# Three products of a swapped projection added in one place, as 256-column matmuls

## The chip, the cores and the metric

The kernel runs on 1 core of one Trainium2 chip. The metric is the device time of one execution in microseconds (us). Before the change it is 2711.26 us, the median of 3 runs (2711.25 to 2711.56).

## The reference, cut to what matters

Two transformer blocks over 256 tokens of width 2048 in float32, one after the other, with a norm between them:

```
x = x + gla(rmsnorm(x)) ; x = x + (relu(rmsnorm(x) @ w_up)**2) @ w_down      # block 1, hidden width 8192
x = rmsnorm(x)
proj = rmsnorm(x) @ w_in_2          # q k v | xr gr | sc_b sc_c sc_x | three gates of 2048
x = x + (g_a*attention + g_b*lru + g_c*shortconv) @ w_out
x = x + (relu(rmsnorm(x) @ w_up_2)**2) @ w_down_2 ; x = rmsnorm(x)
```

Nearly all arithmetic is in the projections, matrix products with weights that are read once from HBM, 499.5 MB in all.

## The kernel before, in words

**Products.** TensorE multiplies in float32r. A float32 operand is split into hi, its rounding to float32r, and lo, what is left; a product is x_hi w_hi + x_hi w_lo + x_lo w_hi. An activation tile holds for each 128-feature group the hi of 256 tokens and then the lo of 256 tokens, side by side and transposed.

**Jobs.** A job is one block of 512 output columns. Its weights stream in chunks of 512 features by 512 columns (1 MB, issued on SP's queue at L181); each chunk is two halves of 256 features. For each half ACT writes hi (`wh`, L204) and DVE lo (`wl`, L205), up to three halves ahead of TensorE. `run()` walks over all halves of all jobs in program order and calls `products()` for each.

**Plain and swapped jobs.** A plain job holds the activations stationary and streams 512 weight columns: for each feature group and each 128 tokens three matmuls of 512 columns, two of them in a row with the same stationary tile. A swapped job holds the weights stationary and streams the activations, so that its output comes out with its 512 columns on the partitions, in four blocks of 128. For each block and each feature group it issues two matmuls: `wh` against hi and lo together (512 columns: x_hi w_hi in the left half of a bank, x_lo w_hi in the right), and `wl` against hi alone (256 columns, added to the left half). A job has four blocks and 16 feature groups, so 64 such pairs. There are 50 swapped jobs: 4 in block 1's mixer (q and k), 16 in each MLP's first projection, 14 in block 2 (short convolution 6, recurrence 4, attention q and k 4). That makes 3200 pairs.

**PSUM.** Accumulators (`acc`) are whole banks, six in rotation: a swapped job takes four, a plain one two. Two more banks serve side work.

**Side work.** Norms, gates, scans and attention are generators that advance one step after each half. A swapped job's generator begins with `g_sum` (L301): for each block ACT copies the right half of the bank to SBUF (L304) and DVE adds it to the left half (L305). What follows depends on the job; in the MLP it is relu and square in one DVE instruction (L608), then the split into hi and lo (L612, L616).

Every engine works through its own queue in program order; all matmuls of the projections have one line (L212).

Of the kernel before, what the change touches and what calls it, by code (L numbers as in the profile page):

```python
# [8 lines left out]
F32 = mybir.dt.float32  # L9
F32R = mybir.dt.float32r  # L10
AF = mybir.ActivationFunctionType
ALU = mybir.AluOpType
# [4 lines left out]
KB = 512  # L17
# [5 lines left out]
NSLOT = 26  # L23


# Every projection runs as a stream of weight tiles through TensorE in float32r.  A float32 operand is
# split exactly into hi = round(w) and lo = round(w - hi); a product is x_hi w_hi + x_hi w_lo + x_lo w_hi.
# An activation tile holds, for two 128-feature groups, [hi of 256 tokens | lo of 256 tokens], transposed.
# A plain job multiplies with the activations stationary and returns [token, 512 columns] in two banks; a
# swapped job holds the weights stationary and returns its columns on partitions, [column, (hi sum | lo sum)].  # L30
# Side work (norms, gates, scans, attention) is written as generators that advance between weight tiles.
class Job:
    def __init__(self, w, kts, act, ev, key, need=None, pre=None, swap=False):
        self.w, self.kts, self.act, self.ev, self.key, self.swap = w, kts, act, ev, key, swap
# [4 lines left out]
def two_blocks(tc, A, out):  # L39
    nc = tc.nc  # L40
    es = ExitStack()
    with es:
# [27 lines left out]
        def flat(ap):  # L70
            return ap.rearrange("p a b -> p (a b)")

        # side work -------------------------------------------------------
        active, gens = [], {}

        def start(key, gen):
# [35 lines left out]
                    drain(rec[1])  # L112
                advance(rec)

        # constants -------------------------------------------------------
        xres = cp.tile([128, 2, D], F32, name="xres")
        cst = cp.tile([128, 128], F32, name="cst")
        ident = cst
# [29 lines left out]
            o = offB[n] + kt  # L148
            return colB[:, o:o + 1]

        # weight stream ---------------------------------------------------
        jobs = []
        chunks, halves = [], []
        st = {"dma": 0, "split": 0}
# [53 lines left out]
                if st["dma"] - ci <= RAW:  # L208
                    dma_chunk()

        def mm(o, l, r, a, b):
            PE.matmul(o, l, r, start=a, stop=b)  # L212

        def products(j, acc, x, wh, wl, first, last, toks=(0, 1)):
            if j.swap:
                for n in range(4):
                    c = slice(n * 128, (n + 1) * 128)
                    for i in range(2):
                        mm(acc[n], wh[:, i, c], flat(x[i]), first and i == 0, False)
                        mm(acc[n][:, 0:256], wl[:, i, c], x[i][:, 0, :], False, last and i == 1)  # L220
            else:
                for i in range(2):
                    a, b = first and i == 0, last and i == 1
                    for t in toks:
                        xh = x[i][:, 0, t * 128:(t + 1) * 128]
                        xl = x[i][:, 1, t * 128:(t + 1) * 128]
                        mm(acc[t], xh, wh[:, i], a, False)
                        mm(acc[t], xh, wl[:, i], False, False)
                        mm(acc[t], xl, wh[:, i], False, b)

        def run():
            acc = None
            for s in range(len(halves)):
                j, ci, h, ks, is_first, is_last = halves[s]
                for k in ks:
                    for key in j.need(k):
                        drain(key)
                if is_first:
                    if j.pre:
                        j.pre()  # L240
                    acc = [ps.tile([128, KB], F32, name="acc", tag="acc", bufs=6) for _ in range(4 if j.swap else 2)]
                look = min(LOOK, 1 + s // 3)
                while st["split"] <= min(s + look, len(halves) - 1):
                    split_half()
                if s == len(halves) - 4:
                    for t in range(2):
                        for q in range(s, s + 4):
                            products(j, acc, [j.act(k) for k in halves[q][3]], *whs[q], False, halves[q][5], (t,))
                        j.ev(acc, t)
                    break  # L250
                wh, wl = whs.pop(s)
                products(j, acc, [j.act(k) for k in ks], wh, wl, is_first, is_last)
                if is_last:
                    start(j.key, j.ev(acc))
                tick()
            while active:
                tick()

        # helpers ---------------------------------------------------------
        def pair_transpose(src, pr, name="tp"):  # L260
            tp = tpt([128, 2, 256], name)
            for i in range(2):
# [35 lines left out]
                if pr == 0:  # L298
                    yield 0

        def g_sum(acc, dst):  # L301
            for n in range(4):
                r = t1("right")
                ACT.activation(r, acc[n][:, 256:512], AF.Copy)  # L304
                V.tensor_tensor(dst[:, n, :], acc[n][:, 0:256], r, op=ALU.add)  # L305

        def over4(ap):
            return ap[:, None, :].to_broadcast([128, 4, 256])
# [48 lines left out]
            T[name] = cp.tile([128, 2, 4], F32, name=name)  # L357
            return T[name]

        # ================= block 1 =======================================  # L360
        w_in = A["gla_w_in"][0]
        xd = A["x"][0].rearrange("(t p) d -> p t d", p=128)

# [31 lines left out]
        def ev_q(hf):  # L395
            def f(acc):
                q = T["qT", hf] = slot([128, 4, 256], F32, "qT")
                g_sum(acc, q)
                yield ("rs1",)
                V.tensor_tensor(q, q, over4(R1q), op=ALU.mult)  # L400
            return f
# [77 lines left out]
        def ev_k(hf):  # L479
            def f(acc):  # L480
                k = T["kT", hf] = slot([128, 4, 256], F32, "kT")
                g_sum(acc, k)
                yield ("glow",)
                V.tensor_tensor(k, k, T["E"][hf], op=ALU.mult)
            return f
# [109 lines left out]
            job(A["gla_w_out"][0], n * KB, 16, acts("o1"), ev_out1(n), ("out1", n), lambda k: (("r", k // 4),))  # L595
        stats("ss2"), keep("rs2", 2), keep("rs2q", 2)

        # ================= mlp ===========================================
        def mlp(tag, w_up, w_down, xname, xkeys, rskey, rsq, ev_last):
            for hf in range(2):  # L600
                for jn in range(8):
                    def ev(acc, hf=hf, jn=jn):
                        y = slot([128, 4, 256], F32, "up")
                        g_sum(acc, y)
                        yield 0
                        for p in range(2):
                            v = flat(y[:, 2 * p:2 * p + 2, :])
                            V.scalar_tensor_tensor(v, v, 0.0, v, op0=ALU.max, op1=ALU.mult)  # L608
                        yield 0
                        for p in range(2):  # L610
                            d = T[tag, hf, 2 * jn + p] = act_tile("h")
                            ACT.activation(d[:, :, 0, :], y[:, 2 * p:2 * p + 2, :], AF.Copy)  # L612
                        yield 0
                        for p in range(2):
                            d = T[tag, hf, 2 * jn + p]
                            V.tensor_tensor(d[:, :, 1, :], y[:, 2 * p:2 * p + 2, :], d[:, :, 0, :].bitcast(F32), op=ALU.subtract)  # L616
                    job(w_up, hf * 4096 + jn * KB, 16, acts(xname), ev, (tag + "up", hf, jn),
                        (lambda k: ((xkeys, k // 4),)) if hf == 0 and jn == 0 else None, swap=True)
                for n in range(4):
                    def lhs(k, hf=hf):  # L620
                        return T[tag, hf, k // 2][:, k % 2]
                    if hf == 0:
                        def ev(acc, n=n):
                            drain(rskey)
                            for t in range(2):
                                V.scalar_tensor_tensor(xblk(t, n), acc[t], rsq[:, t:t + 1], xblk(t, n), op0=ALU.mult, op1=ALU.add)
                            yield 0
                    else:
                        ev = ev_last(n)
                    job(w_down[hf * 4096:(hf + 1) * 4096, :], n * KB, 32, lhs, ev, (tag + "dn", hf, n),  # L630
                        (lambda k, hf=hf: ((tag + "up", hf, k // 4),)) if n == 0 else None,
                        pre=pre_dn.get((tag, hf, n)))
# [42 lines left out]

        mlp("m1", A["mlp_w_up"][0], A["mlp_w_down"][0], "x2", "out1", "rs2", T["rs2q"], ev_last1)

        # ================= block 2 =======================================
        w2 = A["w_in_2"][0]
        X3 = acts("x3")  # L680
        r12 = T["r12"]
# [12 lines left out]
        def ev_cols(name, scale):  # L694
            def f(acc):
                d = slot([128, 4, 256], F32, "col")
                T[name] = d
                g_sum(acc, d)
                yield ("r12",)
                if scale:  # L700
                    V.tensor_tensor(d, d, over4(T[scale]), op=ALU.mult)
            return f

        def ev_sx(b):
            def f(acc):
                bs, cx = T["sb", b], T["sc", b]
                xs = slot([128, 4, 256], F32, "xs")
                g_sum(acc, xs)
                yield ("sc", b)
                yield ("sb", b)  # L710
                V.tensor_tensor(flat(cx), flat(cx), flat(xs), op=ALU.mult)
# [48 lines left out]
        def ev_xr(b):  # L760
            def f(acc):
                xs = slot([128, 4, 256], F32, "xs")
                g_sum(acc, xs)
                yield ("r12",)
                V.tensor_tensor(xs, xs, over4(T["R12"]), op=ALU.mult)
                xc = T["xc", b] = slot([128, 4, 256], F32, "xc")
# [37 lines left out]
        def ev_gr(b):  # L804
            def f(acc):
                gs = slot([128, 4, 256], F32, "gs")
                g_sum(acc, gs)
                yield ("r12",)
                V.tensor_tensor(gs, gs, over4(T["R12"]), op=ALU.mult)
                yield 0  # L810
# [220 lines left out]

        mlp("m2", A["w_mlp_up_2"][0], A["w_mlp_down_2"][0], "x5", "out2", "rs5", T["rs5q"], ev_last2)

        # ================= go ============================================
        plan()
        V.memset(ones, 1.0)
        make_identity(nc, ident)
# [76 lines left out]
```

## Time and profile before

| | |
|---|---|
| median of 3 runs | 2711.26 us |
| profiled execution, first to last instruction (span) | 2709.5 us |
| mean granted TensorE clock | 0.999 of full |
| TensorE matmul (PE) busy | 2696.5 us, 13389 matmuls |
| TensorE weight load (PEld) busy | 2264.6 us, 13389 loads |
| VectorE (DVE) busy | 1601.2 us |
| ScalarE (ACT) busy | 1256.7 us |
| DMA | 511.12 MB, 189 GB/s |

The page gives the profiled execution by its span; the 1.8 us up to the median are outside the first and last instruction. An engine's busy time is the union of its instructions' recorded intervals. Matmuls are pipelined, so a matmul's recorded duration overlaps the next one's: what a matmul costs in a stream is the distance from its start to the next start. A group's row has the line, engine, operation, output<-inputs, shape and count, then busy time, mean duration of one, and the idle time of the engine before it.

### The profile page before, as it was taken

What the parts mean: (1) busy time and instruction counts of PE and PEld (TensorE: products, weight loads), DVE (VectorE), ACT (ScalarE), POOL (GpSimd) and SP (SyncE); (2) the same over time, 40 slices, a digit from 0 to 9 for tenths busy, and PEclk for the clock granted to TensorE, in tenths of its full rate; (3) what the DMA queues carried; (4) which work ended last, traced back from release to release, by engine and by line L of the source; (5) the groups of instructions that cost most, each with busy time, mean ns of one, the idle gap of its engine ahead of it and who ended that gap; (6) DMA issues with size and microseconds to landing.
All of it is one profiled execution on the core that took longest, in us unless ns stands there. A gap on an engine that the chain in (4) does not pass through costs nothing.

```text
span 2709.5 us, 33062 instructions
## 1 busy us (share of the span) xinstructions
PE 2696.5 (100%) x13389; PEld 2264.6 (84%) x13389; DVE 1601.2 (59%) x1958; ACT 1256.7 (46%) x1581; POOL 20.0 (1%) x44
## 2 busy tenths in 40 slices
PE   9999999999999999999999999999999999999998
PEld 8877888888888888888888888888888888888887
DVE  6565655664456655667787556555556654466554
ACT  6444555443344444444555444444454443344443
POOL 0000000000000000000000000000000000000000
PEclk9999999999999999999999999999999999999999
DMA  7454555556565655665556555565555555556564
GB/s 238 156 174 152 175 186 185 186 187 200 188 188 186 201 194 187 201 214 185 185 193 219 187 182 182 193 196 187 186 187 186 187 188 200 187 187 202 188 200 140
DMA packets 256402, 511.12 MB, mean 189 GB/s; under 512 B 10524, under 2 KB 11208, under 8 KB 256120
## 3 DMA queue, kind: packets, MB, share of 16 engines
q1 hardware_dynamic: 253672, 499.50, 56.4%
q0 software_dynamic: 2576, 9.50, 1.1%
q8 instruction: 105, 1.72, 0.3%
q14 instruction: 49, 0.40, 0.0%
HBM read 506.86 MB, written 3.68 MB: 188 GB/s over the span
## 4 chain that ended last, share of the span: by engine, by line
PE 99%; DMA 1%; DVE 0%; issue 0%; ACT 0%; SPq 0%; DVEq 0%; ACTq 0%
PE acc L212 96%; PE tp L264 1%; DMA raw<-in_gla_w_in 0%; PE sc L212 0%; PE po L212 0%; PE gate L212 0%; PE as L212 0%; PE ao L212 0%; DMA xres<-in_x 0%; PE z L212 0%; PE tg L212 0%; PE pT L942 0%; DVE wl L205 0%; DVE oh L549 0%; ACT wh L204 0%
## 5 line engine op out<-in xcount | busy, mean ns | idle before, releaser
L205 DVE TENSOR_TENSOR wl<-raw,wh 128x1024 fp32r<-128x1024 f32 x942 | 1151.5, 1224 | 1019.6 <-ACT wh L204 1016.6
L204 ACT ACTIVATE wh<-raw 128x1024 fp32r<-128x1024 f32 x942 | 996.9, 1059 | 1260.3 <-PE acc L212 1208.9
L212 PE MATMUL acc<-a,wh 128*128 128x512 f32 x3200 | 1135.9, 400 | 0.2 <-DVE a L286 0.2
L212 PE MATMUL acc<-a,wl 128*128 128x256 f32 x3200 | 898.9, 281 | 0.3 <-DVE wl L205 0.3
L212 PEld LDWEIGHTS acc<-a,wh 128*128 128x128 f32 x3200 | 601.9, 188 | 150.7 <-ACT wh L204 0.7
L212 PE MATMUL acc<-wh,h 128*128 128x512 f32 x2048 | 632.9, 389 | 0.0
L212 PE MATMUL acc<-wh,a 128*128 128x512 f32 x1920 | 615.8, 395 | 0.0
L212 PEld LDWEIGHTS acc<-a,wl 128*128 128x128 f32 x3200 | 604.9, 189 | 1.0 <-DVE wl L205 0.6
L212 PEld LDWEIGHTS acc<-wh,h 128*128 128x128 f32 x2048 | 384.5, 188 | 79.8
L212 PEld LDWEIGHTS acc<-wh,a 128*128 128x128 f32 x1920 | 360.4, 188 | 80.0 <-issue 5.3
L212 PE MATMUL acc<-wl,h 128*128 128x512 f32 x1024 | 398.4, 389 | 0.0
L212 PE MATMUL acc<-wl,a 128*128 128x512 f32 x960 | 374.0, 390 | 0.0
L212 PEld LDWEIGHTS acc<-wl,h 128*128 128x128 f32 x1024 | 192.3, 188 | 39.6
L212 PEld LDWEIGHTS acc<-wl,a 128*128 128x128 f32 x960 | 180.4, 188 | 37.7 <-issue 1.9
L304 ACT ACTIVATE right<-acc 128x256 f32<-128x256 f32 x200 | 75.8, 379 | 43.1 <-PE acc L212 42.6
L285 ACT ACTIVATE a<-tp,colB 128x256 fp32r<-128x256 f32 x64 | 29.8, 466 | 43.9 <-DVE a L286 43.9
L305 DVE TENSOR_TENSOR up<-acc,right 128x256 f32<-128x256 f32 x128 | 48.1, 418 | 1.4
L608 DVE SCALAR_TENSOR_TENSOR up<-up 128x512 f32<-128x512 f32 x64 | 41.2, 684 | 0.0
L616 DVE TENSOR_TENSOR h<-up,h 128x512 fp32r<-128x512 f32 x64 | 41.1, 684 | 0.0
L286 DVE SCALAR_TENSOR_TENSOR a<-tp,colB,a 128x256 fp32r<-128x256 f32 x64 | 30.8, 481 | 17.4 <-ACT a L285 17.4
L212 PE MATMUL acc<-wh,yl 128*128 128x512 f32 x128 | 40.9, 393 | 0.0
L212 PE MATMUL acc<-wh,yc 128*128 128x512 f32 x128 | 40.7, 393 | 0.0
(253 smaller groups left out, 928.8 us busy)
## 6 DMA issues: line engine op xcount, KB each, us to landing
raw<-in_w_in SPq DMA_DIRECT2D x112, 1024.0 KB
raw<-in_mlp_w_up SPq DMA_DIRECT2D x64, 1024.0 KB
raw<-in_mlp_w_down SPq DMA_DIRECT2D x64, 1024.0 KB
raw<-in_w_mlp_up SPq DMA_DIRECT2D x64, 1024.0 KB
raw<-in_w_mlp_down SPq DMA_DIRECT2D x64, 1024.0 KB
raw<-in_gla_w_in SPq DMA_DIRECT2D x46, 1024.0 KB
raw<-in_gla_w_out SPq DMA_DIRECT2D x16, 1024.0 KB
raw<-in_w_out SPq DMA_DIRECT2D x16, 1024.0 KB
```

The source lines that it names most:

```text
L204: ACT.activation(flat(wh), flat(src), AF.Copy)
L205: V.tensor_tensor(flat(wl), flat(src), flat(wh.bitcast(F32)), op=ALU.subtract)
L212: PE.matmul(o, l, r, start=a, stop=b)
L264: PE.transpose(tp[:, i, t * 128:(t + 1) * 128], src(t, 2 * pr + i), ident)
L285: ACT.activation(h, src[:, i, :], AF.Copy, scale=col)
L286: V.scalar_tensor_tensor(l, src[:, i, :], col, h.bitcast(F32), op0=ALU.mult, op1=ALU.subtract)
L304: ACT.activation(r, acc[n][:, 256:512], AF.Copy)
L305: V.tensor_tensor(dst[:, n, :], acc[n][:, 0:256], r, op=ALU.add)
L608: V.scalar_tensor_tensor(v, v, 0.0, v, op0=ALU.max, op1=ALU.mult)
L616: V.tensor_tensor(d[:, :, 1, :], y[:, 2 * p:2 * p + 2, :], d[:, :, 0, :].bitcast(F32), op=ALU.subtract)
```

## The change

In a swapped job all three products now go to the same 256 columns of PSUM. For each block and feature group there are three matmuls of 256 columns in place of one of 512 and one of 256: `wh` against hi, `wh` against lo, `wl` against hi. Two blocks share a bank (left and right half), so a job takes two banks instead of four. `start` is set only on the first matmul that touches a bank. `g_sum` with its two instructions for each block becomes `g_take`, one ACT copy of a whole bank for each two blocks. In the MLP that copy applies relu, and the square becomes a plain DVE product. The other edits remove comments.

```diff
-        def mm(o, l, r, a, b):
-            PE.matmul(o, l, r, start=a, stop=b)
+        def mm(o, l, r, a, b, **kw):
+            PE.matmul(o, l, r, start=a, stop=b, **kw)
...
             if j.swap:
                 for n in range(4):
                     c = slice(n * 128, (n + 1) * 128)
+                    o = acc[n // 2][:, (n % 2) * 256:(n % 2 + 1) * 256]
                     for i in range(2):
-                        mm(acc[n], wh[:, i, c], flat(x[i]), first and i == 0, False)
-                        mm(acc[n][:, 0:256], wl[:, i, c], x[i][:, 0, :], False, last and i == 1)
+                        a, b = first and i == 0, last and i == 1
+                        mm(o, wh[:, i, c], x[i][:, 0, :], a and n % 2 == 0, False, skip_group_check=True)
+                        mm(o, wh[:, i, c], x[i][:, 1, :], False, False, skip_group_check=True)
+                        mm(o, wl[:, i, c], x[i][:, 0, :], False, b and n % 2 == 1, skip_group_check=True)
...
-                    acc = [ps.tile([128, KB], F32, name="acc", tag="acc", bufs=6) for _ in range(4 if j.swap else 2)]
+                    acc = [ps.tile([128, KB], F32, name="acc", tag="acc", bufs=6) for _ in range(2)]
...
-        def g_sum(acc, dst):
-            for n in range(4):
-                r = t1("right")
-                ACT.activation(r, acc[n][:, 256:512], AF.Copy)
-                V.tensor_tensor(dst[:, n, :], acc[n][:, 0:256], r, op=ALU.add)
+        def g_take(acc, dst, f=AF.Copy):
+            for p in range(2):
+                ACT.activation(flat(dst[:, 2 * p:2 * p + 2, :]), acc[p], f)
...
-                        g_sum(acc, y)
+                        g_take(acc, y, AF.Relu)
                         yield 0
                         for p in range(2):
                             v = flat(y[:, 2 * p:2 * p + 2, :])
-                            V.scalar_tensor_tensor(v, v, 0.0, v, op0=ALU.max, op1=ALU.mult)
+                            V.tensor_tensor(v, v, v, op=ALU.mult)
```

## Rows read from the trace of the kernel before

**Rows 1.** The page, part 1: busy us (share of span) x instructions.
```profile
PE 2696.5 (100%) x13389; PEld 2264.6 (84%) x13389; DVE 1601.2 (59%) x1958; ACT 1256.7 (46%) x1581; POOL 20.0 (1%) x44
```
**Rows 2.** The page, part 4: the chain of waits, by engine.
```profile
PE 99%; DMA 1%; DVE 0%; issue 0%; ACT 0%; SPq 0%; DVEq 0%; ACTq 0%
```
**Rows 3.** Groups of instructions, all shapes apart, whole span.
```profile
L212 PE MATMUL acc<-a,wh 128*128 128x512 f32 x3200 | 1135.9, 400 | 0.2 <-DVE a L286 0.2
L212 PE MATMUL acc<-a,wl 128*128 128x256 f32 x3200 | 898.9, 281 | 0.3 <-DVE wl L205 0.3
L212 PE MATMUL acc<-wh,h 128*128 128x512 f32 x2048 | 632.9, 389 | 0.0
L212 PEld LDWEIGHTS acc<-wh,h 128*128 128x128 f32 x2048 | 384.5, 188 | 79.8
L304 ACT ACTIVATE right<-acc 128x256 f32<-128x256 f32 x200 | 75.8, 379 | 43.1 <-PE acc L212 42.6
L305 DVE TENSOR_TENSOR up<-acc,right 128x256 f32<-128x256 f32 x128 | 48.1, 418 | 1.4
L608 DVE SCALAR_TENSOR_TENSOR up<-up 128x512 f32<-128x512 f32 x64 | 41.2, 684 | 0.0
L616 DVE TENSOR_TENSOR h<-up,h 128x512 fp32r<-128x512 f32 x64 | 41.1, 684 | 0.0
L276 ACT ACTIVATE a<-tp 128x512 fp32r<-128x512 f32 x8 | 4.7, 582 | 0.0
L328 ACT ACT_TABLE_LOAD x5 | 6.4, 1283 | 0.1
```
**Rows 4.** The chain in order of time, its longest piece of swapped jobs alone: start, length.
```profile
1143.20 155.46 PE acc L212 x880
```
**Rows 5.** Timeline of PE in a swapped job, from 1204.16 us: start, duration.
```profile
1204.16 0.40 PE L212 MATMUL acc<-a,wh 128*128 128x512 f32 x1
1204.40 0.28 PE L212 MATMUL acc<-a,wl 128*128 128x256 f32 x1
1204.52 0.40 PE L212 MATMUL acc<-a,wh 128*128 128x512 f32 x1
1204.76 0.28 PE L212 MATMUL acc<-a,wl 128*128 128x256 f32 x1
1204.87 0.40 PE L212 MATMUL acc<-a,wh 128*128 128x512 f32 x1
1205.10 0.28 PE L212 MATMUL acc<-a,wl 128*128 128x256 f32 x1
1205.22 0.40 PE L212 MATMUL acc<-a,wh 128*128 128x512 f32 x1
```
**Rows 6.** Timeline of PEld (weight loads), the same stretch.
```profile
1204.40 0.19 PEld L212 LDWEIGHTS acc<-a,wh 128*128 128x128 f32 x1
1204.53 0.19 PEld L212 LDWEIGHTS acc<-a,wl 128*128 128x128 f32 x1
1204.76 0.19 PEld L212 LDWEIGHTS acc<-a,wh 128*128 128x128 f32 x1
```
**Rows 7.** Timeline of PE in a plain job, from 700 us.
```profile
700.09 0.39 PE L212 MATMUL acc<-wl,h 128*128 128x512 f32 x1
700.32 0.62 PE L212 MATMUL acc<-wh,h 128*128 128x512 f32 x2
700.77 0.39 PE L212 MATMUL acc<-wl,h 128*128 128x512 f32 x1
```
**Rows 8.** Timeline: four float32 weight loads in a row; float32 matmuls of 256 columns.
```profile
1562.18 0.53 PEld L212 LDWEIGHTS as<-col 128*128 128x128 f32 x4
...
1298.50 0.59 PE L212 MATMUL gate<-xc,wa 128*128 128x256 f32 x2
1298.93 0.59 PE L212 MATMUL gate<-xc,wx 128*128 128x256 f32 x2
```
**Rows 9.** Windows, a stretch of swapped MLP jobs: PE, PEld, DVE, ACT, POOL busy, clock, DMA.
```profile
430.00:590.00 160.00, 160.00 (x907) 138.78 (x906) 97.14 (x117) 77.03 (x101) 0.00 (x0) 1.00 0.59 189
```

More of the change, by code (lines that the diff above doesn't have):

```diff
@@ L397, in f @@
                 q = T["qT", hf] = slot([128, 4, 256], F32, "qT")
-                g_sum(acc, q)
+                g_take(acc, q)
                 yield ("rs1",)
@@ L481, in f @@
                 k = T["kT", hf] = slot([128, 4, 256], F32, "kT")
-                g_sum(acc, k)
+                g_take(acc, k)
                 yield ("glow",)
@@ L697, in f @@
                 T[name] = d
-                g_sum(acc, d)
+                g_take(acc, d)
                 yield ("r12",)
@@ L707, in f @@
                 xs = slot([128, 4, 256], F32, "xs")
-                g_sum(acc, xs)
+                g_take(acc, xs)
                 yield ("sc", b)
@@ L762, in f @@
                 xs = slot([128, 4, 256], F32, "xs")
-                g_sum(acc, xs)
+                g_take(acc, xs)
                 yield ("r12",)
@@ L806, in f @@
                 gs = slot([128, 4, 256], F32, "gs")
-                g_sum(acc, gs)
+                g_take(acc, gs)
                 yield ("r12",)
```

## The prediction, made before the result was known

> **What bounds the kernel now.** I read the page's first part, then its chain of waits, then the groups, and last the timelines of single stretches. The first part has PE busy for all but 13 of 2709.5 us, while DVE and ACT have 41% and 54% of it free [rows 1]. The chain that ended last is 99% PE [rows 2]. In the groups the matmuls of swapped jobs found TensorE idle for 0.5 us in all [rows 3]: neither weights, nor activations, nor a free PSUM bank is waited for. So the end is set by how fast TensorE runs through its queue, and the change is worth what it does to the distance from one matmul's start to the next. Mean durations in the groups (400, 281, 389 ns) are no help there, since neighbours overlap; the timelines are.
>
> In a swapped job, three pairs go from 1204.16 to 1205.22, 1.06 us, so 353.3 ns a pair [rows 5]. The long piece of the chain says the same: 155.46 us for 880 matmuls, 440 pairs, 353.3 ns each [rows 4]. In a plain job three matmuls of 512 columns take 0.68 us (700.09 to 700.77), 226.7 ns each [rows 7]. The granted clock in a stretch of MLP jobs is 1.00, the 2.4 GHz level [rows 9]. A column costs one cycle, since 226.7 ns are 544 cycles for 512 columns. So a plain matmul is 213.3 ns of columns and 13.3 ns of something else, and a pair is 320 ns of columns (768) and 33.3 ns of something else.
>
> **The change, part by part.**
>
> *Matmuls.* 3200 pairs (512 + 256 columns) become 3200 triples (256 + 256 + 256). The columns stay 768; one matmul is added to each pair, with its own weight load: in plain jobs two neighbours share their stationary tile, yet there are 2048 loads for 2048 matmuls [rows 3], so a repeated tile is loaded again. The whole question is what a third matmul with a load of its own costs, at the same number of columns. No row shows a run of 256-column float32r matmuls, so I bound it from three sides.
>
> From below: the distance from a 256-column matmul to the next start is 0.12, 0.11 and 0.12 us in the swapped stream [rows 5], 117 ns. Three of these are 350 ns, 3.3 less than a pair. If 256 columns took half of a plain matmul's time, 113.3 ns, a triple would be 340 ns, 13.3 less.
>
> From above: a pair less a plain matmul of 512 columns is 353.3 - 226.7 = 126.7 ns. If that is what a 256-column matmul with its load really costs, its 117 ns in the timeline is too short and the rest shows up in the 512-column matmul behind it, which takes 0.24, 0.24 and 0.23 us [rows 5] against 0.227 in plain jobs. Three of them are 380 ns, 26.7 more than a pair.
>
> Between: two ways meet at 360. With a fixed 13.3 ns to each float32r matmul, as in plain jobs, 256 columns take 106.7 + 13.3 = 120 ns, a triple 360. Or with 113.3 ns for each 256 columns, a pair is 340 plus 13.3 for its two loads, 6.7 a load; with three loads it is 360 again. I take 360: it is nearest to the longer of the distances in the timeline (0.12), and needs no matmul to be dearer than its like is now. Per triple that is +6.7 ns, and 3200 times that +21.3 us.
>
> The loads themselves are recorded at 0.19 us each and would be 564 ns for three if they excluded each other; they don't: a load starts 0.13 us after the one before [rows 6], and four float32 loads in a row take 0.53 us, so (0.53 - 0.19) / 3 = 113 ns from start to start [rows 8]. That fits under a slot of 120, though barely.
>
> The Trainium skill, "TensorE: Matmul & The Clock Gate", section "LDWEIGHTS (loading the stationary operand)", gives a load of 128 columns about 107 ns whatever it holds. It agrees with the 113 ns of rows 8, and it speaks against this change: a load today has a 512-column stream to hide under every second time, and afterwards never. By it the upper end, 126.7 ns a slot, gains weight; the sum itself does not use it.
>
> *Accumulating in one place.* Three matmuls in a row now add to the same 256 columns. That is done today: `wl` adds to columns that `wh` has just written, and the next pair returns to them 117 ns later. Plain jobs do it three times in a row. No cost.
>
> *PSUM.* Two banks for a job in place of four. TensorE waits for no bank today, so nothing is gained.
>
> *Taking the result out.* 200 ACT copies of 379 ns (75.8 us) and 200 DVE adds (128 of them 48.1 us, 418 ns each [rows 3]; so 83.6) go. 100 ACT copies of 512 columns from PSUM come, at 582 ns by the nearest row, 58.2 us. ACT gains 18 us, DVE 84. Relu moves into ACT's copy; the square stays one DVE instruction of 684 ns, which a two-operand product of that size takes as well [rows 3]. If relu needed a table of its own, two loads of 1283 ns for each of 32 MLP jobs would be 82 us on ACT. All of this lies beside TensorE: in a stretch of MLP jobs ACT is busy 77 of 160 us and DVE 97 [rows 9], and TensorE waits for neither. Worth nothing either way; the cover would be gone only if a half's split came later than TensorE needs it, and it has three halves of eight pairs, 2.8 us each, in hand.
>
> *Ends.* The start, where the first weights arrive, and the last job, a plain one, are untouched.
>
> **Sum.** The profiled span of 2709.5 plus 21.3 is 2730.8 us; with the 1.8 us between span and median, 2732.6.
>
> **The rivals.**
>
> *Faster.* A 256-column float32r matmul costs what its slot in the swapped stream shows, 117 ns, or at best the plain pace, 113.3. Then a triple is 350 (-3.3 ns, -10.7 us, 2700.6) to 340 (-13.3 ns, -42.7 us, 2668.6). For it: those slots are measured, and the odd thing in the stream is its 512-column matmuls, 10 ns slower than in plain jobs; a stream of equal matmuls may lose that. Against it: what is lost behind a 256-column matmul seems to be paid by its neighbour, and all loads would now come at 113 to 117 ns. It decides if the slot is below 117.8 ns. Chance 0.21.
>
> *No change.* The cost follows columns alone, 0.46 ns each (353.3 / 768), whatever they are cut into: 2711. Between the others, chance 0.09.
>
> *A load for each 256 columns is the bound.* 126.7 ns a slot, 380 a triple, +26.7 ns, +85.3 us: 2796.6. For it: the exact difference between the two streams, and that a load (113 ns) is longer than the 106.7 ns of columns it has to hide under. Against it: the 117 ns slots. Chance 0.17.
>
> *The mean overhead stays.* A swapped matmul with its load costs 33.3 / 2 = 16.7 ns beside its columns; a third adds 16.7 ns, triple 370, +53.3 us: 2764.6. For it: it takes the pair whole and needs no story on how the two share. Chance 0.18.
>
> *A third matmul is nearly free.* Float32 matmuls of 256 columns stand 215 ns apart (0.43 us for two [rows 8]), 1.7 ns over 512 cycles: a matmul with its load adds little where the stream is not float32r. With 1.7 ns, +5.4 us, 2716.7. Against it: no float32r stream here is that tight. Chance 0.05, and it lies at the edge of what can be told. The Trainium skill, "TensorE: Matmul & The Clock Gate", section "Back-to-back issue gap", puts the distance at columns / 2.4 + 2.5 ns; by that the extra matmul costs 2.5 ns, +8 us. The plain stream's 226.7 ns against its 215.8 disagrees.
>
> *That the change doesn't do what it says* (the second matmul on the same `wh` reusing its load) is excluded by the 2048 loads above.
>
> **How the numbers follow.** My forecast, 360 ns a triple, has 0.30. Its own range is 2720 to 2745 (358 to 364 ns). With the rest, slower has 0.30 + 0.17 + 0.18 + half of the nearly free case, 0.68; within 0.2% (5.4 us, about what a measurement of this kernel can tell from no change) has 0.09 and the other half, 0.11; faster 0.21. The range that should hold the time 8 times in 10 goes from the upper faster case, 2700, to the bound by loads, 2797, and leaves out the plain pace (340) and anything dearer than 380.
>
> **What would show it.** PE and PEld at 16589 instructions; no `right` copies; starts of `acc<-a,wh` 128x256 and `acc<-a,wl` 128x256 120 ns apart in MLP-up stretches, with PE still at 100% and no new wait of PE. Slots of 113 to 117 ns would make the faster rival right, 123 the mean overhead, 127 the load bound; PEld without idle time between loads would go with the last. The plain stream must stay at 226.7 ns. The prediction is wrong in kind if TensorE starts to wait for ACT or DVE, and wrong in size if the slot is not 120.

## The result, and the profile after

The changed kernel takes 2732.85 us (median of 4 runs, 2732.71 to 2733.12) against 2711.26 before: ratio 1.0079, 95% interval 1.0067 to 1.0091. It is slower by 21.6 us, where 21.3 were forecast (2732.6 us). The spans tell the same: 2731.1 less 2709.5 is 21.6 us.

First part of the page of the changed kernel, then its chain of waits; these answer to [rows 1, 2].

```profile
PE 2718.2 (100%) x16589; PEld 2436.7 (89%) x16589; DVE 1527.3 (56%) x1758; ACT 1244.7 (46%) x1481; POOL 20.1 (1%) x44
...
PE 99%; DVE 0%; ACT 0%; issue 0%; DVEq 0%
```

PE and PEld have 3200 instructions more each; DVE is 74 us less busy and ACT 12 (84 and 18 were forecast), and TensorE still sets the end. The groups that answer to [rows 3]:

```profile
L213 PE MATMUL acc<-a,wh 128*128 128x256 f32 x6400 | 1158.2, 284 | 0.0
L213 PE MATMUL acc<-a,wl 128*128 128x256 f32 x3200 | 906.5, 283 | 0.3 <-DVE wl L206 0.3
L308 ACT ACTIVATE up<-acc 128x512 f32<-128x512 f32 x64 | 38.2, 597 | 42.9 <-PE acc L213 42.9
L611 DVE TENSOR_TENSOR up<-up 128x512 f32<-128x512 f32 x64 | 41.2, 685 | 0.0
```

No idle time ahead of the matmuls, so no new wait. What they cost in a stream is read from the chain in order of time (start, length, count) and from PE's timeline; these answer to [rows 4, 5]:

```profile
1152.06 158.40 PE acc L213 x1320
```

```profile
850.17 0.28 PE L213 MATMUL acc<-a,wl 128*128 128x256 f32 x1
850.29 0.40 PE L213 MATMUL acc<-a,wh 128*128 128x256 f32 x2
850.53 0.28 PE L213 MATMUL acc<-a,wl 128*128 128x256 f32 x1
850.65 0.40 PE L213 MATMUL acc<-a,wh 128*128 128x256 f32 x2
850.89 0.28 PE L213 MATMUL acc<-a,wl 128*128 128x256 f32 x1
```

The piece is the same 440 pairs as in [rows 4], now triples: 158.40 / 440 = 360.0 ns, where a pair took 353.3. In the timeline two triples take 0.72 us (850.17 to 850.89), so 120 ns from start to start. 3200 x 6.7 ns is 21.4 of the 21.6 us. One window in the MLP, answering to [rows 9] (PE, PEld, DVE, ACT, POOL busy, clock, DMA), shows something more:

```profile
430.00:590.00 160.00, 160.00 (x1335) 160.00 (x1335) 84.11 (x84) 74.21 (x84) 0.00 (x0) 1.00 0.61 185
```

PEld, 138.78 of 160 us before, has no idle time left. I had named that as the sign of the rival in which the load is the bound, whose price was 380 ns and not 360. So the number stood, and the reason was open.

### The profile page after: what moved, and what is told of

Same layout as the page of the kernel before. It is cut to its first block, busy times and chain, and to the rows that moved or that the text cites. A ratio compares the mean times of both kernels' runs of the same rounds, so it can differ in the third digit from the quotient of the medians.

```text
span 2731.1 us, 39208 instructions
## 1 busy us (share of the span) xinstructions
PE 2718.2 (100%) x16589; PEld 2436.7 (89%) x16589; DVE 1527.3 (56%) x1758; ACT 1244.7 (46%) x1481; POOL 20.1 (1%) x44
## 4 chain that ended last, share of the span: by engine, by line
PE 99%; DVE 0%; ACT 0%; issue 0%; DVEq 0%
PE acc L213 96%; PE tp L269 1%; PE sc L213 0%; PE po L213 0%; PE gate L213 0%; PE as L213 0%; PE ao L213 0%; PE z L213 0%; PE warm L213 0%; PE tg L213 0%; PE pT L945 0%; DVE wl L206 0%; ACT a L290 0%; DVE oh L552 0%; ACT wh L205 0%
## 5 line engine op out<-in xcount | busy, mean ns | idle before, releaser
L213 PE MATMUL acc<-a,wh 128*128 128x256 f32 x6400 | 1158.2, 284 | 0.0
L213 PEld LDWEIGHTS acc<-a,wh 128*128 128x128 f32 x6400 | 1000.1, 192 | 2.9 <-issue 1.0
L213 PEld LDWEIGHTS acc<-a,wl 128*128 128x128 f32 x3200 | 614.8, 192 | 0.5 <-DVE wl L206 0.5
L308 ACT ACTIVATE up<-acc 128x512 f32<-128x512 f32 x64 | 38.2, 597 | 42.9 <-PE acc L213 42.9
L611 DVE TENSOR_TENSOR up<-up 128x512 f32<-128x512 f32 x64 | 41.2, 685 | 0.0
L213 PE MATMUL acc<-wh,ya 128*128 128x512 f32 x128 | 40.1, 389 | 0.0
```

Of the source, the lines that this page charges most:

```text
L213: PE.matmul(o, l, r, start=a, stop=b, **kw)
L308: ACT.activation(flat(dst[:, 2 * p:2 * p + 2, :]), acc[p], f)
L611: V.tensor_tensor(v, v, v, op=ALU.mult)
```

## The experiments

All times are medians, or one run where no interval stands; "before" beside them was 2711.2 us. Pieces are those of the chain that hold the same 440 pairs or triples.

**The evacuation alone (old_evac).**

```diff
-            for p in range(2):
-                ACT.activation(flat(dst[:, 2 * p:2 * p + 2, :]), acc[p], f)
+            for n in range(4):
+                r, half = t1("right"), acc[n // 2][:, (n % 2) * 256:(n % 2 + 1) * 256]
+                ACT.activation(r, half, f)
+                V.tensor_tensor(dst[:, n, :], half, r, op=ALU.max)
```

> The changed kernel with the evacuation work of before put back: for each of the four blocks an ACT copy of 256 columns (with relu in the MLP) and a DVE instruction over both (a maximum of a value with its own copy), 200 + 200 instructions in place of 100. Theory, ACT and DVE are hidden behind TensorE and the lighter evacuation is worth nothing: 2732.9 us within 2 us. Rival, it gave back part of what the third matmul costs (a free bank or a shorter queue at job ends): slower by more than 5 us, 2738 or more.

Measured 2733.05 us, ratio to before 1.008 (1.0066 to 1.0093), the changed kernel's within its interval. The same window as above:

```profile
430.00:590.00 160.00, 160.00 (x1336) 160.00 (x1334) 94.24 (x112) 77.47 (x98) 0.00 (x0) 1.00 0.61 185
```

DVE is 10 us busier in 160 and TensorE issues as many matmuls. The lighter evacuation is worth nothing.

**The banks alone (bank4).**

```diff
-                    o = acc[n // 2][:, (n % 2) * 256:(n % 2 + 1) * 256]
+                    o = acc[n][:, 0:256]
...
+                ACT.activation(dst[:, n, :], acc[n][:, 0:256], f)
```

> The changed kernel, each block in a bank of its own again (four of six banks for a job, left halves only), taken out by four ACT copies of 256 columns. Theory, sharing a bank is worth nothing: 2733 us, slots 120.0 ns. Rival, two blocks in one bank cost time (TensorE goes on in a bank that ACT waits to read) or gain some (no wait for free banks): 2 us or more away, with a wait of PE at the starts of swapped jobs.

2733.81 us, and its piece is again 158.40 us. Two blocks to a bank cost and bring nothing that one run can tell. What is left of the change is its matmuls.

**Equal sizes, 512 columns (wl512).**

```diff
-                        mm(acc[n][:, 0:256], wl[:, i, c], x[i][:, 0, :], False, last and i == 1)
+                        mm(acc[n], wl[:, i, c], flat(x[i]), False, last and i == 1)
```

> The kernel before, with wl multiplied against hi and lo together (512 columns), so the small product lo times lo is added to the right half and computed besides. All matmuls of a swapped job then have 512 columns, with a load each. Theory (columns + 13.3 ns for each matmul, alternating sizes cost the rest): 226.7 ns from start to start, 453.3 a pair, 3200 x 100 = +320 us, 3031 us. Rival, 512 columns of activations against stationary weights are slower by themselves (the 236 ns that the 512-column matmul takes in the stream of before): 472 ns a pair, +381 us, 3092 us.

It took 3031.92 us. Its piece, 199.50 / 880 = 226.7 ns a matmul, and the timeline of PE have the starts as far apart as in plain jobs:

```profile
1276.63 199.50 PE acc L212 x880
```

```profile
900.39 0.39 PE L212 MATMUL acc<-a,wh 128*128 128x512 f32 x1
900.62 0.39 PE L212 MATMUL acc<-a,wl 128*128 128x512 f32 x1
900.85 0.39 PE L212 MATMUL acc<-a,wh 128*128 128x512 f32 x1
901.07 0.39 PE L212 MATMUL acc<-a,wl 128*128 128x512 f32 x1
901.30 0.39 PE L212 MATMUL acc<-a,wh 128*128 128x512 f32 x1
```

So streaming activations against weights is no slower than the reverse. The 236 ns of the 512s in the stream before come from their neighbours.

**Shorter loads (half_load, two_half, all64_256).** The changed kernel with one, two and three matmuls of a triple on 64 stationary columns (in all64_256 after the first half of each job). These kernels leave out part of the products for the upper 64 output columns of each block, so they serve for timing alone:

```diff
# half_load (two_half: the same on the line of wh against lo too)
-                        mm(o, wl[:, i, c], x[i][:, 0, :], False, b and n % 2 == 1, skip_group_check=True)
+                        mm(o[0:64], wl[:, i, n * 128:n * 128 + 64], x[i][:, 0, :], False, b and n % 2 == 1, skip_group_check=True)
# all64_256
-                    c = slice(n * 128, (n + 1) * 128)
-                    o = acc[n // 2][:, (n % 2) * 256:(n % 2 + 1) * 256]
+                    m = 128 if first else 64
+                    c = slice(n * 128, n * 128 + m)
+                    o = acc[n // 2][0:m, (n % 2) * 256:(n % 2 + 1) * 256]
```

> The changed kernel, with the wl matmul loading only 64 of its 128 stationary columns (the lo part of the weights is left out for the upper 64 output columns of each block). Same number of matmuls, each 256 columns; one load of three is half as long. Theory, the 13.3 ns belong to the matmul and not to its load: all slots stay 120.0 ns, 2732.9 us. Rival, 6.7 ns of each slot are the load's: the slot in which the half load runs falls to about 116.7 ns, 3200 x 3.3 = 11 us, 2722 us.

> The changed kernel, with two of the three matmuls (wh against lo, wl against hi) loading 64 of 128 stationary columns (these two products are left out for the upper 64 output columns of each block). Theory, time follows the loads until the plain pace of 113.3 ns for 256 columns is reached: 340 ns a triple, 2733 - 64 = 2669 us. Rival, one half load in three already took all that loads can give back: 350 ns as with one, 2702 us.

> The changed kernel, with all three matmuls of a triple on 64 stationary columns after the first half of each job (seven eighths of the swapped work leaves out the upper 64 output columns of each block). All loads in the run are alike again, and half as long. Theory, a uniform stream costs its columns plus 13.3 ns whatever is loaded, and mixed loads only disturb it: 120.0 ns a slot, 2733 us. Rival, the 120 ns are set by the full load (111.7 ns measured with 128 columns) and go where all loads are short: 113.3 ns a slot or less, 340 ns a triple or less, 2800 x 20 = 56 us less, 2677 us or below.

Measured 2701.9, 2695.49 and 2679.66 us. The three pieces, one from each kernel in that order:

```profile
1139.27 154.01 PE acc L213 x1320
```

```profile
1136.96 152.54 PE acc L213 x1320
```

```profile
1130.67 150.79 PE acc L213 x1320
```

One half load takes 10 ns off a triple (350.0), three times what the rival there had priced; the second takes only 3 more here (346.7), and nothing in the MLP window 430 to 590 us, where the two kernels issue 1360 and 1359 matmuls; over the whole run it is worth 6.4 us, 2.0 ns a triple. Neither expectation for either run held. With all loads short, the piece still has an eighth of full triples (360), so the rest took (342.7 - 45) / 0.875 = 340 ns, 113.3 a slot. The timeline of PE agrees: 0.34 us from one `wl` to the next.

```profile
850.19 0.28 PE L213 MATMUL acc<-a,wl 128*64 128x256 f32 x1
850.31 0.39 PE L213 MATMUL acc<-a,wh 128*64 128x256 f32 x2
850.53 0.28 PE L213 MATMUL acc<-a,wl 128*64 128x256 f32 x1
850.65 0.39 PE L213 MATMUL acc<-a,wh 128*64 128x256 f32 x2
850.87 0.28 PE L213 MATMUL acc<-a,wl 128*64 128x256 f32 x1
```

My theory that 13.3 ns belong to the matmul whatever it loads is refuted: a uniform stream with short loads runs at 113.3 ns, the plain pace of 226.7 for 512. In a uniform stream the full load under 256 columns costs the other 6.7.

**Is it the load or the smaller matmul? (half512, all64_512).** The same shortening in the stream of 512 columns, where a load has room (edits against the kernel before; their other lines add only an argument):

```diff
# half512
-                        mm(acc[n], wl[:, i, c], flat(x[i]), False, last and i == 1)
+                        mm(acc[n][0:64], wl[:, i, n * 128:n * 128 + 64], flat(x[i]), False, last and i == 1, skip_group_check=True)
# all64_512 (the two lines replaced are those of the kernel before)
...
+                        m = 128 if first else 64
+                        c = slice(n * 128, n * 128 + m)
+                        mm(acc[n][0:m], wh[:, i, c], flat(x[i]), first and i == 0, False, skip_group_check=True)
+                        mm(acc[n][0:m], wl[:, i, c], flat(x[i]), False, last and i == 1, skip_group_check=True)
```

> The kernel with all swapped matmuls of 512 columns (wl against hi and lo), with the wl matmul loading and producing only 64 of its 128 columns (the lo part of the weights is left out for the upper 64 output columns of each block). The 256-column triple had become 10 ns shorter with one such matmul. Theory, the shorter load did that: under 512 columns a load is hidden, so both slots stay 226.7 ns, 3032 us. Rival, a matmul with 64 output columns is itself shorter by about 10 ns: its slot is 217 ns, 3200 x 10 us less, 3000 us.

> The kernel with all swapped matmuls of 512 columns, and all of them on 64 stationary columns after the first half of each job (the upper 64 output columns of each block are left out there). With full loads the slot was 226.7 ns, with full and half loads in turn 231.7. Theory, unlike neighbours cost the 5 ns: with all loads alike 226.7 ns again, 3032 us. Rival 1, short loads themselves cost them: 231.7 or more, 3060 us. Rival 2, the 13.3 ns beside the columns belong to the load and halve with it: 220 ns, 5600 x 6.7 = 37 us less, 2994 us.

Measured 3060.23 and 3050.29 us; pieces of 202.42 and 202.17 us, so 230.0 and 229.7 ns a matmul in this stretch.

```profile
1288.83 202.42 PE acc L212 x880
```

```profile
1283.96 202.17 PE acc L212 x880
```

A matmul with 64 output columns is not shorter in itself: here the stream became 3 ns slower, and it stayed so with all loads alike. So the gain at 256 columns is put down to the load; this is by elimination, at another number of columns. Why short loads cost 3 ns under 512 columns is not explained. "Unlike neighbours" fails as the whole reason, since in all64_512 they are alike. It may be a part: in the MLP jobs the timeline of half512 has ten starts from 900.05 to 902.37 us, 232 ns apart, and that of all64_512 ten from 899.92 to 902.22, 230 ns.

**The load by itself (cols128).**

```diff
-                        mm(o, wh[:, i, c], x[i][:, 0, :], a and n % 2 == 0, False, skip_group_check=True)
+                        for t in range(2):
+                            q = slice(t * 128, (t + 1) * 128)
+                            mm(o[:, q], wh[:, i, c], x[i][:, 0, q], a and n % 2 == 0 and t == 0, False, skip_group_check=True)
...
```

> The changed kernel, each of the three matmuls cut into two of 128 columns, each with its own load of the same weights: the result is the same. It measures what a matmul with its load costs where the load is longer than the columns (53.3 ns). If the load path is what holds 256-column slots at 120 ns, the slot stays 120 ns: 720 ns a triple, 2732.9 + 3200 x 0.36 = 3885 us; at the 113 ns that loads of float32 stood apart in the trace of before: 680 ns, 3757 us. If the matmul has 13.3 ns of its own on top of its columns and loads are not the bound: 66.7 ns, 400 a triple, 2861 us.

3828.53 us, which holds over 200 us at half clock (last section). The piece, at full clock, and the loads in its timeline:

```profile
1669.74 294.75 PE acc L213 x2640
```

```profile
900.11 0.53 PEld L213 LDWEIGHTS acc<-a,wh 128*128 128x128 f32 x4
```

294.75 / 2640 = 111.6 ns a matmul, with 53.3 ns of columns: the load path sets it, at (0.53 - 0.19) / 3 = 113 ns from load to load. A full load needs all but 1.7 ns of the 113.3 that 256 columns take. The Trainium skill, "TensorE: Matmul & The Clock Gate", section "LDWEIGHTS (loading the stationary operand)", puts a load's ns at its columns divided by 1.2, by which 128 columns are an estimate of 107 ns; this stream shows 111.6.

**The order of sizes (sort2, sort8, sort16).** The kernel before, its matmuls sorted by size within a block, within a half, and within a half with the order turned in every second one:

```diff
# sort2: inside the loop over blocks
                     for i in range(2):
                         mm(acc[n], wh[:, i, c], flat(x[i]), first and i == 0, False)
+                    for i in range(2):
                         mm(acc[n][:, 0:256], wl[:, i, c], x[i][:, 0, :], False, last and i == 1)
# sort8: two loops over blocks
+                for n in range(4):
+                    for i in range(2):
+                        mm(acc[n], wh[:, i, cs[n]], flat(x[i]), first and i == 0, False)
+                for n in range(4):
+                    for i in range(2):
+                        mm(acc[n][:, 0:256], wl[:, i, cs[n]], x[i][:, 0, :], False, last and i == 1)
# sort16: big() and small() hold those two loops, j.odd changes with each half
...
+                for part in ((small, big) if j.odd else (big, small)):
+                    part()
```

> The kernel before, with one edit: for each half of a swapped job the eight 512-column matmuls come first and the eight 256-column ones after them, in place of alternating. Same instructions, same sums, two changes of size in 16 matmuls in place of 16. My theory is that every float32r matmul costs its columns plus 13.3 ns (226.7 and 120.0 ns), and that what a pair takes above 346.7 ns (353.3 less 346.7, 6.7 ns) is paid for alternating between sizes: then seven eighths of 3200 x 6.7 = 21.3 us go, about 2692.6 us. Rival 1, 6.7 ns for each weight load on top of 113.3 ns for each 256 columns: loads stay, 2711 us. Rival 2, a change to 512-column matmuls has to settle each time (in the trace of before some ten matmuls of a plain job take about 60 ns more in all after other work): 400 changes of up to 60 ns are 24 us and eat the gain, 2711 to 2716 us.

> The kernel before, its swapped matmuls sorted by size and with the order turned round in every second half: 8 of 512 columns, 8 of 256, then in the next half 8 of 256 and 8 of 512, so that runs are 16 long and there is one change of size each way in two halves. In the run sorted by halves alone the 512s behind a change took 27 ns more in all (233, 236, 228, 232, 231 against 226.7) and the first two 256s 7 ns less than 120. Theory, that is paid for each change of size and not for each matmul: a pair costs 346.7 + 20 / 16 = 347.9 ns, 2711.2 - 3200 x 5.4 = 2694 us. Rival, the 512s catch up on what the run of 256s before them put off, in proportion to its length: then 16 of them put off twice as much, a pair stays at 349.1 ns, 2699 us.

> The kernel before, with the four matmuls of a block sorted by size: 512, 512, 256, 256 in place of 512, 256, 512, 256. Half as many changes of size. Theory, a pair costs 226.7 + 120.0 = 346.7 ns and the 6.7 ns on top are paid for changes of size: half of them stay, 350.0 ns a pair, 2700.5 us. Rival, what comes first after a change is what counts (in the run sorted by halves the first two 512s took 233 and 236 ns, the first two 256s 113 and 119): 350.8 ns a pair, 2703 us. Rival 2, sorting gains only with longer runs: 353.3 ns, 2711 us.

Measured 2698.78 us (ratio 0.9954, 0.9941 to 0.9968), 2695.28 (0.9942, 0.9928 to 0.9956) and, in one run, 2696.1. Their pieces, sort2 first, then sort8 and sort16:

```profile
1137.00 153.26 PE acc L212 x880
```

```profile
1137.93 153.62 PE acc L212 x880
```

```profile
1136.88 153.09 PE acc L212 x880
```

348.3, 349.1 and 347.9 ns a pair. In sort16 the pair is what the theory said, and it beats both kernels; 1.5 us of it are lost again at the start, where sorted matmuls want the lo of the first activations sooner. This line of its waits (engine, line <- releaser, total us, times, longest) shows it:

```profile
PE acc L212 <- DVE a L295: 1.5, 3, 0.5
```

sort8 gained 12.4 us where 18.6 were expected. sort2, with four times the changes of size of sort8, is not slower than it, so a fixed price per change of size is refuted: the strict alternation of 512 and 256 is what costs, and two in a row already remove 5.0 of the 6.7 ns by which a pair exceeds the two uniform streams (226.7 + 120.0). The trace of sort8 shows where a change of size is paid: behind a run of 256s the first two 512s take 233 and 236 ns and the last ones 227; behind a run of 512s the first two 256s take 113 and 119 and all others 120.

## Why the prediction was right, and where it was not

**The bound** held: TensorE's queue, with no wait before or after.

**The third matmul**, +6.7 ns a triple, measured 360.0 less 353.3: the term that carries the sum is right to 0.1 ns. The way to it is right only in part. I had reached 360 in two ways, and the runs separate them. *Columns plus 13.3 ns for each matmul* gives the right number for both uniform streams with full loads (226.7 and 120.0) but is no cause: all64_256 has as many matmuls and runs at 113.3. What stands above one cycle a column is thus no fixed sum: it is 13.3 ns at 512 columns (wl512) and 6.7 at 256 (all64_256, short loads). *113.3 ns for 256 columns plus 6.7 a load* is what all64_256 shows for loads under 256 columns. Its other half, that the pair's 13.3 ns were two loads, is wrong: under 512 columns a full load costs nothing (wl512, 226.7 is twice 113.3), and sorting takes 4 to 5 of the 13.3 away. So the difference came out right though one of its two numbers, the pair, is made of other parts. Counted by the uniform streams it is 340 for columns, 6.7 for the one load under 256 columns, and 6.7 (353.3 less 226.7 and 120.0) for the alternation. By that count the change took the alternation away and put two more loads under 256 columns: -6.7 + 13.3 = +6.7. The forecast had its 6.7 ns a load from another sum and did not know the alternation; that the two terms leave just one load's worth was luck.

**The rival "a load for each 256 columns is the bound"** named the place that the runs found (a full load under 256 columns, 111.6 ns by itself) and mis-sized it. Its 126.7 ns was the pair less a plain matmul, and so held the alternation too; the load's part of it is 120.0. The Trainium skill, "Perfetto Trace Analysis", section "Identifying the Most-Contended Engine", says to judge TensorE's headroom by MFU (the arithmetic done as a share of the peak) and by the busy share of weight loads, rather than by that of matmuls. Here the share of loads went from 87% to 100% in the MLP window while PE stood at 100% in both, so it pointed at the right place. It gives no price, though, and does not show a bound: all64_256, at the plain pace, has nearly the same share in that window:

```profile
430.00:590.00 160.00, 160.00 (x1371) 158.73 (x1370) 89.03 (x89) 78.28 (x89) 0.00 (x0) 1.00 0.63 193
```

A load is recorded at 0.13 us with 64 columns and 0.19 with 128, longer than a slot of 0.113 or 0.120, so the records fill the row in either case.

**The faster rival** fell because the 117 ns slots that it rests on belong to a stream in which every second load lies under 512 columns; with full loads under each, the slot is 120.0. The trace of sort8 bears this out: only the first two 256s behind a 512 are below 120. The mean overhead (370 ns) and the nearly free matmul (355) fell with the same number.

**Costed at nothing:** accumulating in one place (all64_256 does it at the plain pace), the banks (bank4) and the evacuation (old_evac) were right. ACT's copy takes 597 ns where I took 582, and relu needed no table load: the counts of table loads are the same in both traces, 16.

**Two slips** changed no result. The forecast's own range, 2720 to 2745 us, is 356 to 364 ns a triple and not 358 to 364. And the 2048 loads named as proof that a repeated tile is loaded again belong to matmuls whose neighbour before has another tile; the repeat is the `wl` matmul of a plain job, and it does have a load for each of its 1024 matmuls in the MLP (groups of the kernel before):

```profile
L212 PEld LDWEIGHTS acc<-wl,h 128*128 128x128 f32 x1024 | 192.3, 188 | 39.6
```

**Open:** how a full load under 256 columns turns 113.3 into 120.0 when it needs 111.6; why one short load in three gives back 10 ns, and a second one 3 or nothing; and why alternating sizes or shorter loads disturb the 512-column stream. A load of other length inside a fixed matmul could not be had, since a load's columns are the matmul's output columns.

## What to carry to other kernels

At the same number of columns, count the weight loads and what each one lies under: a float32r load of 128 columns took 111.6 ns in a stream bound by loads; by the uniform streams it was free under 512 columns and cost 6.7 ns under 256. Try matmuls of unlike size in runs of two or more rather than in turn; that reorder alone was worth 0.6% here (2711.2 to 2695.3 us in sort16). Before engines beside TensorE are relieved at its expense, check that anything waits for them.

## What the runs showed of the hardware

In cols128, the stretch from 70 to 200 us runs at half clock while matmuls of 128 columns with a load each follow each other without a gap; later jobs of the same kind are at full clock. Windows (PE, PEld, DVE, ACT, POOL busy, clock, DMA):

```profile
70.00:200.00 130.00, 130.00 (x612) 130.00 (x611) 22.40 (x32) 24.46 (x40) 0.23 (x2) 0.50 0.17 52
...
640.00:800.00 160.00, 160.00 (x1435) 160.00 (x1435) 45.18 (x44) 39.18 (x44) 0.00 (x0) 1.00 0.31 99
```

PE's busy share is 100% in both. The granted clock is 0.50 (the 1.2 GHz level) in one and 1.00 in the other, so a busy row alone does not say which clock is granted. A matmul with its load takes 130 / 612 = 0.212 us in the one and 160 / 1435 = 0.111 in the other, so the pace of the loads goes with that clock. The clock is still 0.50 from 200 to 230 us and 0.97 from 230 to 260; from 227.85 us the engine ran sixteen matmuls of another product (`tg`), 512 columns each.
